# A two-layer encoder trunk on one core: sums of the activations built from their two parts in memory, a head's decay gates called behind the scores of the head ahead of it, norm and transposes placed later

## The chip, the cores and the metric

The kernel runs on one core of a Trainium2 chip. The metric is the time of one execution on the device in microseconds (us). Times of before are the median of three runs; one further execution was profiled, and every time of an instruction comes from that one.

## The reference

The input `x` is 512 tokens of 2048 features, with 16 learned meta tokens put ahead of it, so 528 tokens run through two layers:

```
for i in range(2):
    y = rmsnorm(h, pre_norm[i])
    if i == 0: y = attention_mixer(y, ...)   # 16 query heads, 8 key/value heads, 128 wide
    else:      y = gla_mixer(y, ...)         # 4 heads, key 256, value 512 wide
    h = h + rmsnorm(y, post_norm[i])
return h[:, 16:]
```

The second mixer is gated linear attention in both directions. It projects the normed activations to q, k, v, an output gate and two low-rank gates. Each direction's low-rank gate gives a log-decay per token and key feature; its running sum is `b`. A score of a query and a key is the product of `q * exp(b)` and `k * exp(-b)`, under the direction's mask. The sum over the values is normed per head, multiplied with `silu(gate)`, and projected out. All is float32.

## The kernel before

**Two parts.** A float32 product is made of three matmuls of a rounded type (F32R): each operand is split into a high part and a low part (`split`, L134 a copy on ScalarE into the rounded type, L135 a subtraction on VectorE). Weights come from memory as 512 KB units into `wraw` (2 buffers) and are split into `whi` and `wlo` (3 each). The activations that are projected lie in `uh` and `ul`, 16 tiles of 128 features by 528 tokens each. `three` (L156) issues the three matmuls, `project` (L161) a projection to 128 columns: 16 feature tiles by three matmuls for each part of the tokens (`HALVES` are two parts of 264 tokens, `REAL` the 512 without meta tokens). A projection over `HALVES` is 96 matmuls, one over `REAL` 48.

**The planner.** The order in which instructions are called is made by `Clock` (L39). Each k step of a projection advances its time by the planned length of its matmuls (`clk.step`). A side work is a generator: `clk.drive` starts it, each `yield dt` puts its next piece dt later, and it is called between two k steps when its time has come; `clk.after(dt, fn)` does so for one function. `clk.finish(h)` calls all that is due, without matmuls between, until h is done. These are planned times, in what is called planner us below. The call order is the priority of the instructions; the framework that puts them on the engines may pull one ahead that is ready sooner, and weights are called with a priority raised by 400 instructions.

**Norm between the layers.** The last tiles of the first layer's output projection are made for the first half of the tokens and then for the second. `evac` (L793) scales a result into `hs` and adds up its square (L730 on ScalarE, L732 on GpSimd). Behind a half's last tile `mean_rsqrt` (L741) sums over the partitions with a matmul by ones (L744, `ssq`, in the one bank of `ps_t`) and makes `r0`. `residual` (L748) then makes h for one of 16 tiles and one half: it loads the input h (`h0`, 5 buffers), multiplies, adds, stores h to memory (`hf_d`, L754, on GpSimd's queue), and makes `uh` (L755) and `ul` (L756), scaled with the second layer's norm weight. `residuals` (L813) calls those of the first half; `low_rank` (L766), a side work of the next projection group, calls those of the second half. `token_major` (L779) transposes four tiles for 128 tokens into a bank (L785, `ht`), squares it for the second norm (L787) into `hb` (2 buffers), copies it to `hb` (L789) and stores that as `h1_d` from the SP queue (L790). `second_norm` (L844) makes that norm from the squares: `dg`, `mrow`, `r1row`, then the low-rank gates' input (`lt`, allocated as `r0`; `lrf`, L873).

**Sums for the seven products.** Most value columns are projected with seven products in place of eight (`seven`, L218): the feature tiles are two halves and the tokens two halves, and four of the products take sums and differences of activations, T1 to T4. `combine` (L198) makes these for the feature tiles k and k + 8 in eight steps: it loads both from `hf_d` into `x` (4 buffers, of which two exist only once the norm's tiles are gone), scales them with the norm weight (L208, L209 on ScalarE), makes the differences (L211 to L213 on VectorE), and splits the result into `th` and `tl`. Beside it four projections go to memory (`to_dram`, L860): k of head 0 (two, the first one ahead of the building), q of head 0, and the first gate tile of heads 1 and 2; `kq_d` has these in slots 0 to 4. `token_rows` (L888) transposes two value columns (L896, `vps`) and stores them as `v_d` (L901); it is called whole, 1.0 planner us behind its columns.

**GLA heads.** For each head `gates(h)` (L956) makes the running sums (`pz` matmuls L972 into the one bank of `ps_m`, `z` L973, then VectorE's scans L980 to L983), `scores(h, slot)` (L1015) fourteen score blocks (`decayed` L993 makes an operand with exp, product and split; `sm` and `ss` are the matmuls of L1011 to L1013), and `outputs(h, slot)` (L1067) the product with the values, its norm (`sso`, L1095, also in `ps_m`) and the gate. The loop over heads drives `outputs(h - 1)` and `head(h)` (gates, then scores once the outputs and q are done) beside the projections of q, of the next head's k, and of the gate tiles, and calls what is left of `head(h)` at its end. In heads 1 and 2 the first gate tile is loaded (`load_gate`, L1166), the other three are projected.

Of the kernel before, what the change touches and what calls it, by code (L numbers as in the profile page):

```python
# [82 lines left out]
def hybrid_encoder(  # L83
# [21 lines left out]
    hf_d = scratch.tile([KT, P, T], F32, name="hf_d")  # L105
    kq_d = scratch.tile([6, P, T], F32, name="kq_d")
# [91 lines left out]
    def combine(th, tl, xs, src, scale):  # L198

        def load(k):  # L200
            if k < KH:
                x = xs[k % len(xs)]
                nc.sync.dma_start(out=x.rearrange("p (j t) -> p j t", j=2), in_=src[k:k + KH + 1:KH].rearrange("j p t -> p j t"))
        for k in range(len(xs)):
            load(k)
        for k in range(KH):
            x = xs[k % len(xs)]
            A.activation(x[:, :T], x[:, :T], AF.Copy, scale=scale(k))  # L208
            A.activation(x[:, T:], x[:, T:], AF.Copy, scale=scale(k + KH))  # L209
# [5 lines left out]
            load(k + len(xs))  # L215
# [532 lines left out]
    def residual(k, a, b):  # L748
        h0 = t2.tile([P, HALF], F32, tag="h0", name="h0", bufs=5)
# [4 lines left out]
        nc.gpsimd.dma_start(out=hf_d[k][:, a:b], in_=h)  # L754
# [24 lines left out]
    def token_major(k, t):  # L779
# [6 lines left out]
        hb = t2.tile([P, 512], F32, tag="hb", name="hb")[:n]  # L786
# [6 lines left out]
    def evac(ps, a, b):  # L793
        sq = squares(m, ps, a, b)
        if m == KT - 1:
            if a == 0:
                clk.after(2.0, lambda: mean_rsqrt(r0, [acc[:, a:b], sq], a, b))
                clk.after(3.5, lambda: side.append(clk.drive(residuals())))
            else:
                clk.after(1.6, lambda: mean_rsqrt(r0, [acc[:, a:b], sq], a, b))  # L800
# [43 lines left out]
    def second_norm():  # L844
# [5 lines left out]
        for t, c, n in TOK:  # L850
            dg = t2.tile([P, HALF], F32, tag="h0", name="dg", bufs=5)[:, :P]
# [104 lines left out]
    def gates(h):  # L956
# [5 lines left out]
        V.tensor_tensor(ups[32:48], ur, ups[0:16].bitcast(F32), op=ALU.subtract)  # L962
        one = ones[:, 0:1].broadcast_to([P, SEQ])
# [365 lines left out]
```

## Time and profile before

| what | value |
|---|---|
| median of three runs | 1822.78 us (1819.43 to 1823.13) |
| the profiled execution's own time | 1819.71 us |
| its span, first to last instruction | 1818.0 us |
| VectorE, ScalarE, GpSimd busy | 1063.0, 924.8, 199.3 us |
| mean granted clock of TensorE | 0.996 |
| read from and written to memory | 165.47 and 29.08 MB |

In the tables of the profile, PE is TensorE's matmuls, PEld its weight loads, DVE is VectorE, ACT ScalarE, POOL GpSimd and SP the queue that issues most transfers. An instruction's row has the source line, the engine, the operation, the tile written and the tiles read, their shapes, the count, busy us and mean ns, and then the idle time ahead of it with the instruction that ended it. Buffer numbers are left out of names, so `h0_d` and `h1_d` are both `h_d`.

### The profile page before, as it was taken

The page shows a single profiled execution, that of the slowest core. Times are in us where ns is not written, and L with a number is a line of the kernel's source. Part 1 is how long each engine was busy: PE and PEld are TensorE (multiplying, and loading weights), DVE is VectorE, ACT ScalarE, POOL GpSimd, SP SyncE. Part 2 cuts the span into 40 slices and gives each one's busy share as a digit, 9 for nine tenths or more (in the row PEclk, how much of TensorE's full clock was granted, in tenths as well). Part 3 has the DMA queues.
Part 4 walks back from the last instruction along what each step waited for, and adds up shares of the span by engine and source line. Part 5 has one row for each costly group of instructions (what it writes and reads, how often), then busy time and mean ns, then how long its engine had stood idle before and what let it go on. Part 6 is the DMA issues. An engine that isn't in the chain of part 4 may idle for free.

```text
span 1818.0 us, 32105 instructions
## 1 busy us (share of the span) xinstructions
PE 1777.5 (98%) x12711; PEld 1670.0 (92%) x12711; DVE 1063.0 (58%) x2053; ACT 924.8 (51%) x1869; POOL 199.3 (11%) x255
## 2 busy tenths in 40 slices
PE   8999999999999999999999999999999999999998
PEld 8899999999999999999999899988888888888886
DVE  5786656656565656622255667658585866854224
ACT  4554544444445454533346634459585766953221
POOL 3211111111111111111131001110000000000000
PEclk9999999999999999999999999999999999999999
DMA  8322232223333332523457644343233332344323
GB/s 254 119 59 83 82 88 82 89 83 89 84 92 86 91 112 79 171 86 90 116 165 234 191 120 117 106 135 88 77 105 88 103 93 85 101 139 170 96 93 127
DMA packets 271095, 203.13 MB, mean 112 GB/s; under 512 B 10172, under 2 KB 240640, under 8 KB 270416
## 3 DMA queue, kind: packets, MB, share of 16 engines
q1 hardware_dynamic: 262832, 175.35, 33.0%
q0 software_dynamic: 8112, 25.73, 3.8%
q8 instruction: 100, 1.64, 0.4%
q14 instruction: 51, 0.42, 0.1%
HBM read 165.47 MB, written 29.08 MB: 107 GB/s over the span
## 4 chain that ended last, share of the span: by engine, by line
PE 62%; issue 31%; POOL 3%; DVE 2%; DMA 1%; ACT 1%; SPq 0%; POOLq 0%; DVEq 0%; ACTq 0%
PE pp L157 14%; PE pp L159 14%; PE pp L158 14%; PE f L1243 2%; PE f L1241 2%; PE f L1242 2%; PE pT L581 2%; POOL v_d L901 1%; PE s L562 1%; PE s L563 1%; PE s L564 1%; PE o L602 1%; PE o L601 1%; PE o L603 1%; POOL hf_d L754 1%
## 5 line engine op out<-in xcount | busy, mean ns | idle before, releaser
L157 PE MATMUL pp<-uh,whi 128*128 128x264 f32 (+1 forms) x2640 | 803.6, 305 | 0.3 <-ACT sq L302 0.3
L158 PE MATMUL pp<-ul,whi 128*128 128x264 f32 (+1 forms) x2640 | 794.4, 301 | 0.4 <-DVE ul L429 0.4
L159 PE MATMUL pp<-uh,wlo 128*128 128x264 f32 (+1 forms) x2640 | 794.3, 301 | 0.3 <-POOL wlo L368 0.3
L159 PEld LDWEIGHTS pp<-uh,wlo 128*128 128x128 f32 x2640 | 498.1, 189 | 16.9 <-POOL wlo L368 0.6
L157 PEld LDWEIGHTS pp<-uh,whi 128*128 128x128 f32 x2640 | 497.7, 189 | 17.2 <-ACT st L900 0.8
L158 PEld LDWEIGHTS pp<-ul,whi 128*128 128x128 f32 x2640 | 498.6, 189 | 14.2 <-DVE ul L429 0.6
L135 DVE TENSOR_TENSOR wlo<-wraw,whi 128x1024 fp32r<-128x1024 f32 (+1 forms) x245 | 298.3, 1219 | 345.6 <-ACT whi L134 345.2
L134 ACT CAST whi<-wraw 128x1024 fp32r<-128x1024 f32 (+1 forms) x245 | 254.9, 1042 | 353.5 <-PE pp L158 197.6
L571 ACT ACTIVATE pn<-s,mx 128x528 f32<-128x528 f32 (+1 forms) x72 | 50.3, 698 | 88.5 <-DVE mx L568 62.9
L1243 PE MATMUL f<-whi,ul 128*128 128x512 f32 x192 | 75.6, 394 | 0.0
L1241 PE MATMUL f<-whi,uh 128*128 128x512 f32 x192 | 75.5, 393 | 0.0
L1242 PE MATMUL f<-wlo,uh 128*128 128x512 f32 x192 | 75.3, 392 | 0.0
L314 POOL TENSOR_TENSOR qw<-qw,cos 128x528 f32<-128x528 f32 x24 | 31.9, 1327 | 372.9 <-DMA qs<-qw 315.6
L567 DVE TENSOR_REDUCE mx<-s 128x1 f32<-128x528 f32 (+1 forms) x72 | 50.7, 705 | 18.4 <-PE s L564 17.2
L241 PE MATMUL pp<-th,whi 128*128 128x264 f32 x192 | 54.6, 284 | 0.0
L242 PE MATMUL pp<-tl,whi 128*128 128x264 f32 x192 | 54.6, 284 | 0.0
L243 PE MATMUL pp<-th,wlo 128*128 128x264 f32 x192 | 54.3, 283 | 0.0
L324 DVE TENSOR_TENSOR qw<-qw,qs 128x528 f32<-128x528 f32 x24 | 17.0, 706 | 60.1 <-POOL qs L315 60.1
L134 ACT CAST whi<-x 128x1024 fp32r<-128x1024 f32 x27 | 28.3, 1048 | 43.3 <-PE pp L242 21.4
L586 DVE TENSOR_TENSOR pl<-pT,ph 128x512 fp32r<-128x512 f32 (+1 forms) x80 | 47.4, 592 | 4.8 <-ACT ph L585 3.8
L585 ACT CAST ph<-pT 128x512 fp32r<-128x512 f32 (+1 forms) x80 | 40.6, 507 | 16.5 <-PE pT L581 10.4
L1104 POOL DMA_DIRECT2D og_d<-og x24 | 12.8, 540 | 326.7 <-DVE og L1102 326.7
(374 smaller groups left out, 3358.1 us busy)
## 6 DMA issues: line engine op xcount, KB each, us to landing
wraw<-in_attn_w_in_dram SPq DMA_DIRECT2D x94, 512.0 KB, 4.0
wraw<-in_gla_w_in_dram SPq DMA_DIRECT2D x81, 512.0 KB, 3.9
wraw<-in_attn_w_out_dram SPq DMA_DIRECT2D x32, 512.0 KB, 3.9
wraw<-in_gla_w_out_dram SPq DMA_DIRECT2D x32, 512.0 KB, 3.8
x<-in_gla_w_in_dram SPq DMA_DIRECT2D x15, 512.0 KB, 4.2
qs<-qw SPq DMA_DIRECT2D x96, 66.0 KB, 3.0
h<-h_d SPq DMA_DIRECT2D x32, 132.0 KB, 3.6
hf_d<-h POOLq DMA_DIRECT2D x32, 132.0 KB, 3.3
```

What stands on the lines that cost most here:

```text
L134: A.copy(hi, src)
L135: V.tensor_tensor(lo, src, hi.bitcast(F32), op=ALU.subtract)
L157: PE.matmul(ps, wh, uh[:, k, a:b], start=first, stop=False)
L158: PE.matmul(ps, wh, ul[:, k, a:b], start=False, stop=False)
L159: PE.matmul(ps, wl, uh[:, k, a:b], start=False, stop=last)
L241: PE.matmul(ps, w[0][:, k], bh[:, k], start=k == 0, stop=False)
L242: PE.matmul(ps, w[0][:, k], bl[:, k], start=False, stop=False)
L243: PE.matmul(ps, w[1][:, k], bh[:, k], start=False, stop=k == KH - 1)
L567: V.reduce_max(mx, s, axis=AX.XY)
L1241: PE.matmul(ps, uh[:, k, ts], wh[:, kk], start=(k == 0), stop=False)
L1242: PE.matmul(ps, uh[:, k, ts], wl[:, kk], start=False, stop=False)
L1243: PE.matmul(ps, ul[:, k, ts], wh[:, kk], start=False, stop=(k == KT - 1))
```

## The change

- `combine` no longer loads from memory: `x` is the sum of the two parts `uh` and `ul` of tiles k and k + 8, in one VectorE addition of 128 x 1056. The loads, the two scalings and, in `residual`, the store of h to `hf_d` go.
- The first gate tile of head 2 is projected in its head like the others; `kq_d` has four slots, and only head 1 loads its gate tile.
- `h0` has 4 buffers in place of 5, `hb` 3 in place of 2.
- `mean_rsqrt` is called 3.5 (was 2.0) and 3.2 (was 1.6) planner us behind its half, the residuals 5.0 (was 3.5).
- `token_rows` is a side work with 2.5 planner us ahead of each of its three pieces.
- `gates` waits 2.0 more behind its first copies, `scores` 1.5 more at its two first items, `outputs` 3.0 (was 1.0) ahead of `sso`.
- One generator `heads` makes gates and scores of all heads, with a slot of 4.0 (3.3 in head 3, was 3.4); the loop waits for the scores of head h - 1 when it begins head h, and starts its outputs then.

```diff
-    def combine(th, tl, xs, src, scale):
-
-        def load(k):
-            if k < KH:
-                x = xs[k % len(xs)]
-                nc.sync.dma_start(out=x.rearrange("p (j t) -> p j t", j=2), in_=src[k:k + KH + 1:KH].rearrange("j p t -> p j t"))
-        for k in range(len(xs)):
-            load(k)
+    def combine(th, tl, xs):
+
         for k in range(KH):
             x = xs[k % len(xs)]
-            A.activation(x[:, :T], x[:, :T], AF.Copy, scale=scale(k))
-            A.activation(x[:, T:], x[:, T:], AF.Copy, scale=scale(k + KH))
+            u = [t[:, k:k + KH + 1:KH].bitcast(F32) for t in (uh, ul)]
+            V.tensor_tensor(x.rearrange("p (j t) -> p j t", j=2), *u, op=ALU.add)
...
             split(th[:, k], tl[:, k], x)
-            load(k + len(xs))
             yield 2.4
...
     def residual(k, a, b):
-        h0 = t2.tile([P, HALF], F32, tag="h0", name="h0", bufs=5)
+        h0 = t2.tile([P, HALF], F32, tag="h0", name="h0", bufs=4)
...
-        nc.gpsimd.dma_start(out=hf_d[k][:, a:b], in_=h)
...
-        hb = t2.tile([P, 512], F32, tag="hb", name="hb")[:n]
+        hb = t2.tile([P, 512], F32, tag="hb", name="hb", bufs=3)[:n]
...
             if a == 0:
-                clk.after(2.0, lambda: mean_rsqrt(r0, [acc[:, a:b], sq], a, b))
-                clk.after(3.5, lambda: side.append(clk.drive(residuals())))
+                clk.after(3.5, lambda: mean_rsqrt(r0, [acc[:, a:b], sq], a, b))
+                clk.after(5.0, lambda: side.append(clk.drive(residuals())))
             else:
-                clk.after(1.6, lambda: mean_rsqrt(r0, [acc[:, a:b], sq], a, b))
+                clk.after(3.2, lambda: mean_rsqrt(r0, [acc[:, a:b], sq], a, b))
...
         for ts in ((0, 1), (2, 3), (4,)):
+            yield 2.5
             ps = ps_v.tile([P, 512], F32, tag="v", name="vps")
...
-    built = clk.drive(combine(th, tl, quarters, hf_d, lambda k: col(PRE + KT + k)))
-    clk.after(1.0, lambda ys=ys: token_rows(ys, 0))
+    built = clk.drive(combine(th, tl, quarters))
+    clk.drive(token_rows(ys, 0))
...
-    for n, h in ((3, 1), (4, 2)):
-        to_dram(n, 4096 + h * 512, 1.0, REAL)
+    to_dram(3, 4096 + 512, 1.0, REAL)
...
-        clk.after(1.0, lambda ys=ys, vc=vc: token_rows(ys, vc))
+        clk.drive(token_rows(ys, vc))
...
         V.tensor_tensor(ups[32:48], ur, ups[0:16].bitcast(F32), op=ALU.subtract)
+        yield 2.0
...
                 if d == "m":
                     made = (decayed(kf, bf, cf, 4, -1.0, SEQ, META, "km"), decayed(qf, bf, None, 4, 1.0, c, n, "q"))
+                    yield 1.5
...
-            yield 1.0
+            yield 3.0
             PE.matmul(ps, ones, acc[:, :256], start=True, stop=True)
...
-    def head(h, before):
-
-        yield from gates(h)
-        while not (before["done"] and have["q"]):
-            yield 0.5
-        side = [clk.drive(load_v(h))]
-        if 0 < h < 3:
-            side.append(clk.drive(load_gate(h)))
-        yield from scores(h, 3.4)
-        while not all(s["done"] for s in side):
-            yield 0.5
-
+    def heads():
+
+        for h in range(G_HEADS):
+            yield from gates(h)
+            while not have[h]:
+                yield 0.5
+            side = [clk.drive(load_v(h))]
+            if h == 1:
+                side.append(clk.drive(load_gate(h)))
+            yield from scores(h, 3.3 if h == 3 else 4.0)
+            while not all(s["done"] for s in side):
+                yield 0.5
+            done[h] = True
+
+    have, done = [False] * G_HEADS, [False] * G_HEADS
+    sc = clk.drive(heads())
     for h in range(G_HEADS):
-        have = {"q": False}
-        before = clk.drive(outputs(h - 1, 3.6)) if h else {"done": True}
-        sc = clk.drive(head(h, before))
+        if h:
+            while not done[h - 1]:
+                clk.pop()
+            before = clk.drive(outputs(h - 1, 3.6))
...
-        have["q"] = True
-        clk.finish(*([before] if h else []))
+        if h:
+            clk.finish(before)
+        have[h] = True
...
-        for i in range(1 if 0 < h < 3 else 0, 4):
+        for i in range(1 if h == 1 else 0, 4):
...
-        clk.finish(sc)
+    clk.finish(sc)
     clk.flush()
```

More of the change, by code (lines that the diff above doesn't have):

```diff
@@ L104, in hybrid_encoder @@
     h1_d = scratch.tile([4, P, D], F32, name="h1_d")
-    hf_d = scratch.tile([KT, P, T], F32, name="hf_d")
-    kq_d = scratch.tile([6, P, T], F32, name="kq_d")
+    kq_d = scratch.tile([4, P, T], F32, name="kq_d")
     v_d = scratch.tile([5, P, D], F32, name="v_d")
@@ L850, in second_norm @@
         for t, c, n in TOK:
-            dg = t2.tile([P, HALF], F32, tag="h0", name="dg", bufs=5)[:, :P]
+            dg = t2.tile([P, HALF], F32, tag="h0", name="dg", bufs=4)[:, :P]
             V.tensor_scalar(dg, ident, r1col[:, t:t + 1], None, op0=ALU.mult)
@@ L1167, in load_gate @@
         gr = g2.tile([P, SEQ], F32, tag="gr", name="gr", bufs=1)
-        nc.sync.dma_start(out=gr, in_=kq_d[2 + h][:, :SEQ])
+        nc.sync.dma_start(out=gr, in_=kq_d[3][:, :SEQ])
         yield 4.0
```

## The prediction

> **What bounds the kernel now.** I read the page first, then TensorE's waits, then the windows around the largest of them, then what the other engines did there. Span and busy time are these:
>
> ```profile
> span 1818.0 us, 32105 instructions
> PE 1777.5 (98%) x12711; PEld 1670.0 (92%) x12711; DVE 1063.0 (58%) x2053; ACT 924.8 (51%) x1869; POOL 199.3 (11%) x255
> ```
>
> TensorE is busy 1777.5 of 1818.0 us. A group of matmuls by itself shows how dense that is (columns of this view: window, its length, then busy us and count of PE, PEld, DVE, ACT and POOL, granted clock, DMA share, GB/s):
>
> ```profile
> 810.00:855.00 45.00, 45.00 (x372) 45.00 (x371) 9.81 (x8) 13.59 (x23) 6.77 (x7) 1.00 0.33 94
> ```
>
> 45.00 us hold 372 matmuls of 264 columns, one each 121 ns, at full clock. Work is not removed from TensorE by this change (a 48-matmul projection only moves), so what can be won is what TensorE waits for (columns: us in total, times, longest):
>
> ```profile
> PE vps L896 <- DVE y L248: 3.6, 5, 1.1
> PE ssq L744 <- issue: 2.7, 1, 2.7
> PE sso L1095 <- ACT z L973: 2.1, 3, 0.7
> PE sso L1095 <- DVE acc L1092: 2.1, 2, 1.1
> PE sm L1012 <- DVE lq L135: 2.1, 3, 1.0
> PE ht L785 <- ACT hb L787: 2.0, 1, 2.0
> PE mrow L854 <- DVE dg L852: 1.3, 1, 1.3
> PE mrow L854 <- DVE r L858: 1.0, 1, 1.0
> PE pz L972 <- DVE ups L962: 0.8, 1, 0.8
> PE plr L769 <- ACT hb L789: 0.8, 1, 0.8
> PE pz L972 <- ACT z L973: 0.8, 2, 0.5
> PE pz L972 <- DVE r L1097: 0.6, 1, 0.6
> PE ht L785 <- ACT hb L789: 0.5, 1, 0.5
> PE sso L1095 <- DVE lkm L135: 0.4, 1, 0.4
> PE ss L1011 <- ACT hq L134: 0.4, 1, 0.4
> ```
>
> All of these lie between the first layer's norm and the last GLA head, and they sum to 21.2 us. The wait of an instruction is counted from the modelled end of the one ahead (0.28 us after its start, below), while the next could have followed after 0.12 us; so a wait costs 0.16 us more than its row says.
>
> **The change, part by part.** *Third `hb` buffer, no `hf_d`.* Here is what stands behind the `ssq`, `ht`, `plr` and `mrow` waits:
>
> ```profile
> 944.65 0.60 PE L785 MATMUL ht<-ident,h 128*128 128x128 f32 x4
> 947.46 0.28 PE L158 MATMUL g<-ul,whi 128*128 128x264 f32 x1
> 950.45 0.69 PE L744 MATMUL ssq<-acc,ones 128*128 128x264 f32 x2 [2.70 <-issue]
> 948.24 0.60 ACT L787 ACTIVATE hb<-ht 128x512 f32<-128x512 f32 x1 [1.87 <-DMA h_d<-hb]
> 949.76 0.59 ACT L789 COPY hb<-ht 128x512 f32<-128x512 f32 x1
> 998.63 0.59 ACT L787 ACTIVATE hb<-ht 16x512 f32<-16x512 f32 x1 [3.18 <-DMA h_d<-hb]
> DMA to landing us min/median/max: 2.4/4.1/6.4
> 947.50:950.00 2.50, 0.25 (x3) 0.03 (x1) 0.60 (x3) 1.76 (x4) 0.54 (x1) 1.00 1.04 385
> 950.00:952.50 2.50, 2.05 (x10) 1.86 (x11) 2.50 (x5) 2.50 (x8) 0.54 (x1) 0.86 0.97 355
> 952.50:955.00 2.50, 2.50 (x14) 2.50 (x13) 1.74 (x5) 2.10 (x7) 0.00 (x0) 0.50 0.91 245
> 1002.50:1005.00 2.50, 2.12 (x6) 1.30 (x7) 1.09 (x3) 1.39 (x5) 0.72 (x2) 0.60 0.00 0
> 1005.00:1007.50 2.50, 2.50 (x17) 2.50 (x17) 0.85 (x2) 1.48 (x4) 0.56 (x2) 0.72 0.30 105
> ```
>
> ScalarE's squares of the token-major norm stood 1.87 us at 948.24 until a store of `hb` had landed (median 4.1 us, up to 6.4, with the DMA engines at a share of 1.04). Their bank is the one that `ssq` needs; the copy that empties it starts at 949.76, and `ssq` starts at 950.45, after 2.70 us. At 998.63 the same wait takes 3.18 us, with the second norm, hence `mrow`, behind it. A third buffer lets a burst of three pass without a landing, and 32 stores of `hf_d` no longer share the DMA engines. `mean_rsqrt` placed 1.6 planner us later gives the sums that much more; the residuals start 1.5 later, but VectorE's idle 1.9 us of 947.5 to 950 take that up. One `h0` buffer less may hold a residual back by a landing. So of ssq 2.7, ht 2.0 and 0.5, plr 0.8 (6.0 us) I take 5.0 and leave 1.0 for what is late next, the residuals on VectorE with that buffer. Of `mrow` the 1.3 us for `dg` go; the 1.0 us for `r` stays, because copy and product follow the matmul as before. Gain 6.3.
>
> After both waits the granted clock falls: 0.86 and 0.50, then 0.60 and 0.72, which is (0.14 x 2.5 + 0.50 x 2.5) = 1.6 us lost and (0.40 x 2.5 + 0.28 x 2.5) = 1.7 us, of the second of which some 0.4 us fall into the wait for `r`. Without the long waits I count 1.6 + 1.3 = 2.9 us won. [...] The trace halves it after 2.70 us without a start, so I keep the term.
>
> *`token_rows` in pieces, 2.5, 5.0 and 7.5 planner us behind its columns.* The transposes now wait for the last addition of `y` five times, 3.6 us. Two and a half planner us are over twice the longest, 1.1. All of it goes; the last call, in the flush, is not moved by it. Its stores on POOL's queue spread likewise, with nobody waiting for them. Gain 3.6.
>
> *Placing in the GLA heads.* This row shows the kind of wait, a `sm` matmul that stands for the split of its operand:
>
> ```profile
> 1439.59 0.29 PE L1012 MATMUL sm<-lq,hkm 128*16 128x256 f32 x1 [0.96 <-DVE lq L135]
> ```
>
> The 1.5 us for the first score item exceed the longest `sm` wait (1.0): 2.1 us go. The 2.0 us behind `ups` cover 0.8. The extra 2.0 us ahead of `sso` cover `acc` 2.1 and `lkm` 0.4. But `sso` of a first half waits for `z`, whose bank it shares: by the yields it comes 0.6 planner us after a `pz` (8.2 against 7.6) and will again (10.2 against 9.6), as both are moved by 2.0. So 2.1 stays, and pz for `z` 0.8 and ss 0.4 too. With pz for `r` 0.6 that is 6.0 us touched; I take 5.0.
>
> Tails: 15 of the waits that go (vps 5, sm 3, sso 3, pz 2, ssq, mrow) by 0.16 are 2.4 us. **Won: 6.3 + 2.9 + 3.6 + 5.0 + 2.4 = 20.2 us.**
>
> *Sums from memory.* These are the durations, the stretch from where the splits of the sums can start (the second `lrf`) to the end of the first product that reads them, and one of 512-column matmuls alone:
>
> ```profile
> L208 ACT ACTIVATE x<-x,cols 128x528 f32<-128x528 f32 x8 | 5.9, 734 | 7.6 <-DMA x<-hf_d 7.6
> L209 ACT ACTIVATE x<-x,cols 128x528 f32<-128x528 f32 x8 | 5.8, 727 | 0.0
> L135 DVE TENSOR_TENSOR tl<-x,th 128x1056 fp32r<-128x1056 f32 x8 | 10.0, 1255 | 3.5 <-ACT th L134 3.4
> L211 DVE TENSOR_TENSOR x<-x 128x528 f32<-128x528 f32 x6 | 4.1, 703 | 2.0 <-ACT x L209 2.0
> L135 DVE TENSOR_TENSOR wlo<-wraw,whi 128x1024 fp32r<-128x1024 f32 x9 | 11.0, 1219 | 1.7 <-ACT whi L134 1.7
> L865 DVE SCALAR_TENSOR_TENSOR y<-pp,r1row 128x512 f32<-128x512 f32 (+1 forms) x5 | 2.9, 582 | 0.0
> 1012.00:1063.40 51.40, 51.40 (x293) 45.03 (x293) 37.67 (x47) 27.75 (x37) 3.25 (x6) 1.00 0.65 195
> 1710.00:1755.00 45.00, 45.00 (x197) 36.68 (x196) 12.47 (x12) 11.71 (x17) 0.00 (x0) 1.00 0.30 94
> ```
>
> POOL's queue loses 32 stores, SP's eight loads and ScalarE 11.7 us; none of them ends a wait of TensorE here. VectorE gains eight additions of 128x1056. The trace has none; the nearest row is `tl`, the same size, 1.255 us, so 10.0 us. That needs room, since one projection that hid the building leaves: 197 matmuls in 45.00 us are 0.228 each, 48 of them 10.9. The window holds 37.67 us of VectorE work in 51.40. Afterwards: + 10.0, less the two additions that can run ahead of it on the two buffers that exist early (before, too, only 6 of 8 `L211` lie in it), less two weight splits 2.4 and one evacuation 0.7: 42.1 us in 51.4 - 10.9 = 40.5. VectorE is over by 1.6 us even if never idle; its groups show 7.2 us idle ahead of `tl`, `L211` and `wlo` there, part of it for the scaling that goes. TensorE will wait here, where nothing waits now: between 0 (the product walks through `th` in order and may start early) and 1.6 + 7.2 = 8.8. I take 4.0, nearer to the full queue than to the idle rows. Later products catch up.
>
> *Heads.* The planner's own arithmetic: scores take 15 x 4.0 + 2 x 1.5 = 63.0 planner us behind 22.8 of gates, 85.8, while the projections of head 0 and of head 1 amount to 73.6. So gates don't come earlier than now, and some 12.2 planner us of scores, three items, are called at once ahead of the next head's projections, twice. (Heads 2 and 3: under 2.) Queued behind them in priority are q's matmuls, `outputs` and the next gates. In the trace the order of calls isn't that on TensorE: at 947.46 runs a matmul of the group, behind the transposes of 944.65 and ahead of `ssq`, though `finish` calls `ssq` before the group. So q fills the holes, and what is left are waits like `sm` and `ss`, 0.4 to 1.0 each. Bounds: 0, and two times 12.2 x 1.05 (228 ns where the planner counts 216) = 25.7 if nothing fills. I take 3.0, six items by half a microsecond. The gate tile made in head 2 costs nothing there: the same 48 matmuls, and one load less on SP's queue.
>
> **Sum: 20.2 - 4.0 - 3.0 = 13.2 us won.** The profiled execution took 1819.71 us (span 1818.0 and 1.7 around it), so 1806.5; the median of the three is 1822.78, 3.1 us more, so 1809.6 on that scale.
>
> **Rivals.** *Nothing waits at the places that I price* (no wait at the seam, no hole at the heads): 20.2 won, 1802.6. For it: ScalarE, which VectorE waits for at the seam, loses its scaling. Against: 42.1 in 40.5. *Placing does little*: the order follows readiness, and the waits that only placing touches (3.6 + 5.0 + 2.4 = 11.0) return. Then 20.2 - 11.0 - 7.0 = 2.2 won, 1820.6. Against it: those waits repeat at 0.7 to 1.1 us each, smaller than the shifts. *Slower: the three items stand alone.* If TensorE really sits through the called-at-once scores at both boundaries, 25.7 takes the place of 3.0: 9.5 lost, 1832.3. It decides from 16.2 us for both, 8.1 each. For it speaks that ScalarE is near its limit in head 0's scores already:
>
> ```profile
> 1215.00:1260.00 45.00, 44.22 (x266) 38.01 (x266) 40.27 (x80) 41.92 (x100) 0.00 (x0) 1.00 0.34 96
> ```
>
> 41.92 of 45 us; against it the interleaving above, and that wider slots lighten just this.
>
> **How the numbers follow.** Forecast 0.65, no new waits 0.18, placing does little 0.10, slower 0.07. No change is within 0.2%, 3.6 us, about what a measurement can tell here. Forecast and the first rival are faster, with 0.02 of the third case: 0.85; same 0.08; slower 0.07. The likeliest gives 1809.6. The low end is all won plus 2 of the 3.3 us that I leave: 1800.6. Seam 8.8 with heads 7.6 would leave 3.8 won, 1819.0; the high end reaches to the case behind that, 1820.6.
>
> **What would show it.** Right: `vps`, `ssq`, `ht` and `sm` vanish from the waits, no `hb` square waits for its store, the clock stays 1.00 around 950 and 1003, `sso` for `z` stays, and a wait for `tl` appears at the first `th` product. Wrong: `vps` or `sm` still there with the same length; TensorE idle for over 8 us at a head's boundary; or `th` waits of 10 us, which would mean that VectorE is the bound from there on.

## The result and the profile after

| | median | lowest to highest | runs |
|---|---|---|---|
| before | 1821.32 us | 1819.43 to 1823.13 | 4 |
| after | 1810.31 us | 1806.41 to 1811.77 | 4 |

The ratio is 0.9936, with a 95% interval of 0.9916 to 0.9956. The kernel became 11.0 us faster, between 8.0 and 15.3 us by the interval. The forecast was 13.2 us won. The profiled execution of after took 1810.19 us, and its page begins so (busy us, share and count of each engine):

```profile
span 1808.5 us, 31995 instructions
...
PE 1774.5 (98%) x12711; PEld 1671.9 (92%) x12711; DVE 1072.4 (59%) x2061; ACT 914.9 (51%) x1853; POOL 180.6 (10%) x222
```

The span is 9.5 us shorter than before. TensorE runs the same 12711 matmuls; its busy time is 3.0 us less (1777.5 to 1774.5) and its idle time 6.5 us less (40.5 to 34.0), so about two thirds of the gain in the span are waiting that is gone. VectorE has 9.4 us more, mostly the eight additions (10.0); ScalarE has 9.9 less, mostly the scalings (11.7); GpSimd's part is 18.7 less, mostly the issues of the stores (32 of 0.54 us, 17.3). What TensorE waits for between the norm and the last head is now this (us in total, times, longest):

```profile
PE sso L1088 <- ACT z L965: 5.7, 6, 1.8
...
PE ss L1003 <- ACT hq L133: 2.4, 2, 1.2
PE ht L776 <- DVE h L745: 2.0, 2, 1.7
...
PE vps L1109 <- ACT vt L1103: 1.1, 1, 1.1
...
PE plr L760 <- ACT hb L780: 1.0, 1, 1.0
PE pz L964 <- ACT z L965: 0.8, 2, 0.5
PE sm L1004 <- DVE lq L134: 0.8, 2, 0.4
PE pz L964 <- DVE ups L953: 0.6, 1, 0.6
...
PE ht L776 <- ACT hb L778: 0.6, 1, 0.6
...
PE sm L1003 <- ACT hq L133: 0.3, 1, 0.3
```

Line numbers have moved by 7 to 9 in this part of the code: L1088 is `sso`, L1003 and L1004 are score matmuls, L776 is `ht`, L888 the transposes of `token_rows`. Gone are `vps` for `y` (3.6), `ssq` (2.7), `mrow` for `dg` and `r` (2.3), and `sso` for `acc` and `lkm` (2.5). `ht` for the square (L787 before, L778 now) fell from 2.0 to 0.6. New or longer are `sso` for `z` (2.1 to 5.7, from three times to six), `ss` for `hq` (0.4 to 2.4) and `ht` for h itself (0 to 2.0).

These are windows at the places that were shown of before (columns as there: PE, PEld, DVE, ACT, POOL, granted clock, DMA share, GB/s). The first two are the first norm's, then the second norm, the building of the sums, and two places in the heads:

```profile
947.50:950.00 2.50, 2.19 (x16) 1.91 (x16) 2.50 (x8) 2.46 (x7) 0.00 (x0) 1.00 0.82 243
950.00:952.50 2.50, 2.50 (x21) 2.38 (x20) 2.26 (x7) 2.33 (x7) 0.00 (x0) 1.00 0.97 280
1000.00:1002.50 2.50, 2.50 (x23) 2.50 (x22) 1.14 (x2) 1.05 (x1) 0.00 (x0) 1.00 0.00 0
1003.90:1044.30 40.40, 40.40 (x245) 36.14 (x246) 40.18 (x50) 18.87 (x24) 3.78 (x7) 1.00 0.46 134
1261.00:1263.00 2.00, 1.45 (x6) 1.27 (x7) 1.89 (x5) 1.32 (x3) 0.00 (x0) 0.71 0.38 91
1263.00:1265.00 2.00, 2.00 (x11) 2.00 (x11) 0.52 (x2) 0.55 (x2) 0.00 (x0) 0.50 0.63 188
1370.00:1372.00 2.00, 1.60 (x8) 1.48 (x9) 1.89 (x4) 1.18 (x3) 0.00 (x0) 0.77 0.39 96
```

The clock stays at 1.00 through both norms. In the building VectorE is busy 40.18 of 40.40 us, and TensorE 40.40 of 40.40: VectorE is as full as forecast, and nobody waits for it. In the heads the clock now falls to half twice, at places where it was full before.

This table sets the profiled executions side by side, stage by stage, in us between the starts of TensorE's instructions. The projection that moved from the building into head 2 is 48 x 0.228 = 10.9 us; the last column takes it into account.

| stage | before | after | won |
|---|---|---|---|
| first softmax score to last `lrf` (layer 1, norm) | 928.93 | 920.72 | 8.2 |
| last `lrf` to first `th` product (building) | 48.66 | 37.64 | 11.0, less 10.9 moved: 0.1 |
| first to last `th` product (seven products) | 123.58 | 119.39 | 4.2 |
| last `th` product to first `pz` | 22.47 | 22.30 | 0.2 |
| first `pz` to first `pf` (heads) | 417.65 | 431.54 | -13.9, plus 10.9 moved: -3.0 |
| first `pf` to the end (`pf` is the last projection's first tile) | 194.01 | 194.09 | -0.1 |

The gain lies in the norm and in the seven products. The heads look 3 us worse in this pair of profiles. The two stretches at half clock, 3.41 us each and so 1.7 us lost each, are 3.4 us of that; the experiments show what else is the pair.

### The profile page after: what moved, and what is told of

Read it like the earlier page. It is cut to its first block, busy times and chain, and to the rows that moved or that the text cites. A ratio compares the mean times of both kernels' runs of the same rounds, so it can differ in the third digit from the quotient of the medians.

```text
span 1808.5 us, 31995 instructions
## 1 busy us (share of the span) xinstructions
PE 1774.5 (98%) x12711; PEld 1671.9 (92%) x12711; DVE 1072.4 (59%) x2061; ACT 914.9 (51%) x1853; POOL 180.6 (10%) x222
## 4 chain that ended last, share of the span: by engine, by line
PE 62%; issue 28%; DVE 3%; ACT 2%; POOL 2%; DMA 2%; SPq 0%; POOLq 0%; DVEq 0%; ACTq 0%
PE pp L156 14%; PE pp L158 14%; PE pp L157 13%; PE f L1242 2%; PE f L1240 2%; PE f L1241 2%; PE pT L573 2%; PE s L554 1%; PE s L556 1%; PE s L555 1%; POOL v_d L893 1%; PE o L594 1%; ACT whi L133 1%; PE o L593 1%; PE o L595 1%
## 5 line engine op out<-in xcount | busy, mean ns | idle before, releaser
L134 DVE TENSOR_TENSOR wlo<-x,whi 128x1024 fp32r<-128x1024 f32 x27 | 33.0, 1222 | 19.5 <-ACT whi L133 19.5
```

The source lines that it names most:

```text
L134: V.tensor_tensor(lo, src, hi.bitcast(F32), op=ALU.subtract)
```

## Experiments

Each kernel ran three rounds beside the kernel before on the same chip. In the table, "norm" is the first stage of the table above, "building", "seven" and "heads" are its second, third and fifth; times are of the profiled executions, one for each kernel.

| kernel | ratio to before (95%) | norm | building | seven | heads |
|---|---|---|---|---|---|
| before | 1 | 928.9 | 48.7 | 123.6 | 417.7 |
| after | 0.9936 (0.9916 to 0.9956) | 920.7 | 37.6 | 119.4 | 431.5 |
| 1 before, third `hb` | 0.9985 (0.9975 to 0.9995) | 927.0 | 49.3 | 128.1 | 419.2 |
| 2 before, sums from the parts | 0.9999 (0.9988 to 1.0011) | 928.6 | 48.7 | 122.2 | 424.4 |
| 3 after, two `hb` | 0.9964 (0.9951 to 0.9977) | 931.2 | 37.5 | 119.4 | 430.7 |
| 4 after, norm as early as before | 0.9923 (0.9909 to 0.9938) | 920.0 | 37.6 | 119.7 | 432.1 |
| 5 after, `token_rows` whole | 0.9946 (0.9926 to 0.9967) | 922.2 | 37.6 | 122.4 | 429.4 |
| 6 after, additions twice | 0.9989 (0.9978 to 1.0001) | 922.8 | 42.3 | 123.7 | 432.2 |
| 7 after, heads as before | 0.9937 (0.9923 to 0.9952) | 924.0 | 37.6 | 119.5 | 432.5 |
| 8 after, gate tile by memory | 0.9958 (0.9941 to 0.9975) | 922.2 | 48.8 | 119.3 | 422.2 |
| 9 after, shorter slot | 0.9916 (0.9901 to 0.9931) | 922.4 | 37.6 | 119.5 | 428.8 |
| 10 after, `sso` in another bank | 0.9923 (0.9904 to 0.9941) | 922.7 | 37.6 | 119.5 | 432.7 |
| 11 = 4 and 9 | 0.9904 (0.9887 to 0.9920) | 919.8 | 37.6 | 119.7 | 428.9 |
| 12 = 4, 10 and later operands | 0.9879 (0.9864 to 0.9893) | 920.9 | 37.6 | 119.7 | 424.6 |

**1. The third buffer alone**, in the kernel before.

```diff
-        h0 = t2.tile([P, HALF], F32, tag="h0", name="h0", bufs=5)
+        h0 = t2.tile([P, HALF], F32, tag="h0", name="h0", bufs=4)
...
-        hb = t2.tile([P, 512], F32, tag="hb", name="hb")[:n]
+        hb = t2.tile([P, 512], F32, tag="hb", name="hb", bufs=3)[:n]
```

> The kernel before with a third hb buffer (and h0 at 4) and nothing else of the change. Theory 'buffer': the norm stage wins because a square no longer waits for the store of an hb tile; then the waits ssq 2.7, ht 2.5 and mrow dg 1.3 go, the clock stays full around 950 and 1003, and the time is 6 to 8 us under before, some 1814. Rival 'traffic': the stores of hf_d made the landings late, and the third buffer only helps with them gone; then hb squares still wait several us, and the gain is under 3 us.

The ratio is 0.9985, and the norm stage is 2.0 us shorter, not 8. The squares wait only 0.2 us for their stores (8.5 before), yet TensorE's two long waits are there as before, `ssq` at 951.55 and `ht` at 978.28. This is ScalarE's order of work in that kernel ahead of each of them (start, duration, then the wait), and TensorE's waits:

```profile
947.52 0.63 ACT L787 ACTIVATE hb<-ht 128x512 f32<-128x512 f32 x1
...
949.92 1.04 ACT L134 CAST whi<-wraw 128x1024 fp32r<-128x1024 f32 x1 [1.69 <-DMA wraw<-in_gla_w_in_dram]
950.87 0.58 ACT L789 COPY hb<-ht 128x512 f32<-128x512 f32 x1
...
974.76 0.74 ACT L208 ACTIVATE x<-x,cols 128x528 f32<-128x528 f32 x1 [1.46 <-DMA x<-hf_d]
```
```profile
PE ht L785 <- ACT hb L787: 2.8, 1, 2.8
...
PE ssq L744 <- issue: 2.5, 1, 2.5
```

The square starts without a wait at 947.52. Behind it in ScalarE's queue stands the split of a weight unit, whose transfer lands late (1.69 us), and the copy that empties the bank for `ssq` stands behind that. Ahead of the second wait, ScalarE stands 1.46 us for a load of the sums' building into `x`, and the square that empties the bank for `ht` comes behind it, at 977.57. So a landing that ScalarE no longer waits for at one instruction is followed by one that it waits for at the next. The clock fell to half behind both waits (stretches from 952.41 and 979.72; the granted clock is 0.50 in 952.5 to 955 and in 980 to 982.5). In this profile the seven products are 4.6 us longer than in before: the longest wait of `vps` is 2.3 us, and another stretch at half clock follows it (the mean granted clock of the whole profile is 0.994, that of before 0.996).

**2. The sums alone**, in the kernel before: `combine` as in after, no `hf_d`, two `hb`.

```diff
-        nc.gpsimd.dma_start(out=hf_d[k][:, a:b], in_=h)
...
-    built = clk.drive(combine(th, tl, quarters, hf_d, lambda k: col(PRE + KT + k)))
+    built = clk.drive(combine(th, tl, quarters))
```

> The kernel before with combine's sums from uh and ul, and no hf_d; two hb buffers, all placing as before, four projections beside the building. 'Buffer': the waits of hb squares for their stores stay (8.5 us of ScalarE before), gain under 3 us. 'Traffic': landings fall well under 4.1 us, the waits go, gain 5 to 8 us. Both: no wait at the first th product, since VectorE has 37.7 + 7.5 us of work in 51.4.

No change in time: 0.9999. ScalarE's squares wait as long for their own stores as before, with 32 stores fewer on the DMA engines (us, times):

```profile
  DMA h_d<-hb: 9.2, 5
...
DMA to landing us min/median/max: 2.1/3.2/6.5
```

The median landing is 3.2 us here and was 4.1, but the longest is 6.5 and was 6.4, and two buffers don't outlast that. The building took 48.7 us with the additions in it and 48.7 without, so nothing waits at the seam while the fourth projection still covers it. The load into `x` that held up ScalarE in run 1 (and for 1.41 us at 972.32 in before) is gone, and the longest `ht` wait is 0.5 us in place of 2.0. In the heads, whose code is that of before, this profile has one `sm` wait of 4.6 us and a stretch of 6.8 us at half clock that begins in it (the granted clock from 1180 to 1625 is 0.99, in before 1.00); why was not found.

**3. After with two `hb` buffers.**

```diff
-        hb = t2.tile([P, 512], F32, tag="hb", name="hb", bufs=3)[:n]
+        hb = t2.tile([P, 512], F32, tag="hb", name="hb", bufs=2)[:n]
```

> The changed kernel with two hb buffers. 'Pair': hb squares wait for stores again and 5 us or more of the 8.2 in that stretch are lost. 'Placing': about 2 us are lost, as much as the buffer won alone. In both the stretch from second lrf to the first th product and all behind it stay as they are.

The norm is 10.5 us longer than in after, and the ratio goes back to 0.9964. The store waits are back in full:

```profile
  DMA h_d<-hb: 9.4, 6
...
DMA to landing us min/median/max: 2.1/3.9/6.4
```

Runs 1 to 3 together: the buffer alone is worth 2.0 us in this stage, the absent stores and loads alone 0.3, and both (run 4, below, has just these two in the norm) 928.9 - 920.0 = 8.9. Neither is enough by itself; they work as a pair. Run 1's trace has both kinds of landing behind which the waits then stood, a weight unit's and a load's into `x`; how much each of them is worth was not separated.

**4. After with the norm placed as early as before.**

```diff
-                clk.after(3.5, lambda: mean_rsqrt(r0, [acc[:, a:b], sq], a, b))
-                clk.after(5.0, lambda: side.append(clk.drive(residuals())))
+                clk.after(2.0, lambda: mean_rsqrt(r0, [acc[:, a:b], sq], a, b))
+                clk.after(3.5, lambda: side.append(clk.drive(residuals())))
             else:
-                clk.after(3.2, lambda: mean_rsqrt(r0, [acc[:, a:b], sq], a, b))
+                clk.after(1.6, lambda: mean_rsqrt(r0, [acc[:, a:b], sq], a, b))
```

> The changed kernel with the norm's sums and the residuals called as early as before (2.0, 3.5 and 1.6). From the first softmax score to the second lrf the kernel before takes 928.9 us, the changed one 920.7; a third hb buffer alone gave 2.0 of these 8.2, the sums alone 0.3. Theory 'pair': third buffer and absent stores together give the rest, the later calls nothing; the stretch stays within 1 us of 920.7. Rival 'placing': the later calls give it; the stretch goes back to some 926, the time rises by 4 to 6 us.

The norm is not longer: 920.0. One wait stands in it, in place of after's `ht` for h, `ht` for `hb` and `plr`:

```profile
PE ssq L736 <- issue: 1.6, 1, 1.6
```

With the late placing, `ssq` finds its sums ready and the residuals, now 1.5 later, make `ht` wait. The seven kernels with the late placing, two-part sums and three buffers (after, 5 to 10) took 920.7 to 924.0, 922.4 in the mean; the three with the early placing (4, 11, 12) 919.8 to 920.9, 920.2 in the mean. So the later placing of the norm costs some 2 us in this stage, of which about 0.7 are the clock: three of the seven profiles (6, 9, 10), and none of the three, have a stretch at half clock near 955, taken at 1.7 us each. The two groups touch (after has 920.7), so the size is uncertain. In the time of the whole kernel this lies within the intervals.

**5. After with `token_rows` whole**, 1.0 behind its columns as before.

```diff
+        yield 1.0
         c = slice(vc * P, (vc + 2) * P)
         for ts in ((0, 1), (2, 3), (4,)):
-            yield 2.5
```

> The changed kernel with token_rows called whole, 1.0 planner us behind its columns, as before. Theory 'late addition': the five vps waits for y come back (3.6 us, 4.4 with tails), the seven-product stretch grows from 119.4 to 123.6 us and the time by 4. Rival 'given back': the later stretches take up what is lost; the time moves by less than 1.5 us.

The seven products are 3.0 us longer, 122.4 against 119.4, and the wait that had vanished is there again, five times:

```profile
PE vps L888 <- DVE y L240: 2.4, 5, 0.7
```

In the time of the whole kernel (0.9946) this lies within the intervals.

**6. After with every addition made twice**, 8 x 1.25 = 10.0 us more on VectorE in the building.

```diff
-            V.tensor_tensor(x.rearrange("p (j t) -> p j t", j=2), *u, op=ALU.add)
+            for _ in range(2):
+                V.tensor_tensor(x.rearrange("p (j t) -> p j t", j=2), *u, op=ALU.add)
```

> The changed kernel with each of the eight additions of uh and ul done twice (same result, 10.0 us more of VectorE, of which two additions lie ahead of the building). VectorE is busy 40.2 of the 40.4 us from the second lrf to the end of the first th product, and TensorE does not wait there. Theory 'edge': that stretch is full, so 7.5 us more on it delay the first th products by 5 to 8 us. Rival 'slack': much of what VectorE does there is work for later that moves back; TensorE waits under 2 us.

The building is 4.7 us longer and the seven products 4.3, together 9.0 for the 10.0 added. These are TensorE's waits in that stretch, VectorE's group of additions (busy us, mean ns, idle ahead), the window behind the longest wait, and two instructions of ScalarE ahead of it:

```profile
PE pp L234 <- ACT y L258: 4.5, 1, 4.5
...
PE pp L235 <- DVE tl L134: 0.9, 1, 0.9
```
```profile
L203 DVE TENSOR_TENSOR x<-uh,ul 128x1056 f32<-128x1056 f32 x12 | 15.0, 1250 | 0.0
```
```profile
1045.00:1047.00 2.00, 1.81 (x8) 1.81 (x9) 2.00 (x3) 0.14 (x1) 0.00 (x0) 0.50 0.84 225
```
```profile
1041.93 1.99 ACT L133 CAST whi<-wraw 128x1024 fp32r<-128x1024 f32 x2 [2.44 <-DVE wraw L228]
...
1044.77 0.37 ACT L258 COPY y<-pp 128x264 f32<-128x264 f32 x1
```

The waits for `y` and `tl`, with 0.5 us for `th`, are 5.9 us; behind the longest comes a stretch of 6.8 us at half clock, which costs 3.4. The theory of the edge holds in the time lost. The longest wait is not for a sum, though: by its row the first `th` product waits for ScalarE's copy L258, which starts at 1044.77 behind the casts of weights, and the first of these waited 2.44 us for a sum of weights on VectorE (L228). By its parts, of the 10.0 us added 4.1 still found room: 2.5 ahead of the building (12 of the 16 additions lie in it, 6 of 8 in after) and 1.6 in it. The rest stands in TensorE's way, with the clock on top of it. In after the same additions have no idle time ahead of them, and the last `tl` is made late. These are the group, the first `th` product, the last `tl`, and what TensorE runs then:

```profile
L202 DVE TENSOR_TENSOR x<-uh,ul 128x1056 f32<-128x1056 f32 x6 | 7.5, 1250 | 0.0
```
```profile
1041.14 0.29 PE L233 MATMUL pp<-th,whi 128*128 128x264 f32 x1
...
1043.69 0.44 PE L233 MATMUL pp<-th,whi 128*128 128x264 f32 x2
...
1045.07 0.41 PE L234 MATMUL pp<-tl,whi 128*128 128x264 f32 x2
```
```profile
1043.71 1.25 DVE L134 TENSOR_TENSOR tl<-x,th 128x1056 fp32r<-128x1056 f32 x1
```

The first `th` product starts at 1041.14, and the last `tl` ends at 1043.71 + 1.25 = 1044.96, 3.8 us behind that start. The product takes the eight pieces in turn, three matmuls each, and comes to the last one at 1043.69, before its `tl` is made. There its first matmul and the first of the next product run one behind the other (x2 in the row); nine more of the next product follow, and the one that needs the last `tl` runs at 1045.07, beside the next product's (x2 again). So two things cover the late `tl`: the order of reading, and some 1.2 us of the next product put in between.

**7. After with the heads' loop and yields of before**, and the gate tile still made in head 2.

```diff
-    def heads():
-
-        for h in range(G_HEADS):
-            yield from gates(h)
-            while not have[h]:
-                yield 0.5
...
+    def head(h, before):
+
+        yield from gates(h)
+        while not (before["done"] and have["q"]):
+            yield 0.5
...
+        yield from scores(h, 3.4)
```

> The changed kernel with the heads as before: one generator for each head, slots of 3.4, the shorter yields ahead of pz, sm and sso; sums, buffers, token_rows and the gate tile of head 2 stay as changed. From the first pz to the first output matmul the kernel before takes 417.7 us with one projection (10.9) less, which makes 428.6; the changed one takes 431.5. Theory 'heads lose': the stretch is 428 to 429 and the kernel 2 to 4 us faster than the changed one. Rival 'heads win': the waits that placing removed (sm 2.1, acc 2.1) return on top of today's, and it is 3 us slower.

The ratio stays at 0.9937 and the heads take 432.5 us, 1.0 more than in after, so the new loop with its placing loses nothing by itself (that the heads lose, as supposed until then, falls) and, in the stage's time, gains next to nothing. The waits change hands:

```profile
PE sm L1002 <- ACT hq L133: 2.2, 1, 2.2
...
PE sso L1086 <- ACT z L964: 2.1, 3, 0.7
PE pz L963 <- DVE ups L953: 2.0, 2, 1.3
PE sso L1086 <- DVE acc L1083: 1.8, 2, 1.0
```

**8. After with head 2's first gate tile by memory**, as before, and a slot of 3.2 in head 2 so that its planned sum fits.

```diff
-    to_dram(3, 4096 + 512, 1.0, REAL)
+    for n, h in ((3, 1), (4, 2)):
+        to_dram(n, 4096 + h * 512, 1.0, REAL)
...
-            if h == 1:
+            if 0 < h < 3:
                 side.append(clk.drive(load_gate(h)))
-            yield from scores(h, 3.3 if h == 3 else 4.0)
+            yield from scores(h, (4.0, 4.0, 3.2, 3.3)[h])
```

> The changed kernel with head 2's first gate tile made beside the state's building again, written to memory and read back ahead of head 2, as the kernel before does; its 48 matmuls leave head 1's softmax and stand between the last norm product and the first th product (head 2's step of the schedule is 3.2 there, so that its planned sum fits). Theory 'the tile is neutral': the 10.9 us only change place: last norm product to first th product 48.6 us instead of 37.6, the heads 431.5 - 10.9 = 420.6 us instead of 431.5, and the time is the changed kernel's within 1.5 us. Rival 'the tile costs in the heads': its matmuls and the conversions behind them crowd the heads, which come out 3 to 4 us below that, at about 417, since the kernel before has 417.65 there although with the old order of the heads and the tile in them they took 432.5, and the time is 3 to 4 us less than the changed kernel's.

The building is 48.8 us again, and the heads 422.2, nearer to 420.6 (neutral) than to 417. That the tile costs in the heads falls; where it is made doesn't matter to within the spread. The ratio, 0.9958, is if anything on the slower side of after's, and the intervals overlap.

Heads with the old loop, the tile's 10.9 us taken out, took 417.7, 419.2, 424.4 (2) and 421.6 (7), 420.7 in the mean. With the new loop they took 420.6, 419.7, 421.1, 418.5, 421.2 (after, 3, 4, 5, 6) and 422.2 (8), 420.5 in the mean. With 1.7 us taken off for each 3.41 us at half clock in the heads, the means are 419.8 and 419.1. The heads are neutral; that the profile of before had 417.7, the best of its four, and that of after two stretches at half clock, made them look 3 us worse in the pair.

**9. After with a slot of 3.2 in heads 0 and 1**, so that the scores' planned time fits beside the projections and no items are left for one call at the boundary.

```diff
-            yield from scores(h, 3.3 if h == 3 else 4.0)
+            yield from scores(h, (3.2, 3.2, 4.0, 3.3)[h])
```

> The changed kernel with a slot of 3.2 in heads 0 and 1, so that gates and scores (22.8 + 51.0 planner us) end with the head's projections (73.6) and no items are left to be called at once. Theory 'called at once': the two ss waits of 1.2 us and the two half-clock stretches of 3.4 us at 1261 and 1371 go, 4 to 6 us under the changed kernel, some 1805. Rival 'crowding': ScalarE and VectorE are the limit of the scores, and closer slots bring ss and sm waits of the same sum elsewhere; within 2 us of the changed kernel.

The heads are 2.8 us shorter, and the granted clock in them is 1.00 (from 1180 to 1625), where after has 0.99. The waits there:

```profile
PE sso L1088 <- ACT z L965: 6.1, 6, 1.8
...
PE sm L1004 <- DVE lq L134: 1.3, 3, 0.4
PE sm L1003 <- ACT hq L133: 1.3, 3, 0.6
...
PE ss L1003 <- ACT hq L133: 0.7, 1, 0.7
```

`ss` falls from 2.4 to 0.7, and `sm` rises from 1.1 to 2.6 in its place. Of the 2.8 us, the waits give little; the two half-clock stretches behind after's `ss` waits, of about 3.4 us each at half speed, were worth 1.7 each. That is not the edit's alone: in runs 3 and 5 the two `ss` waits are there, the granted clock in the heads is 1.00 in both, and they take 430.7 and 429.4, so without the clock the shorter slot wins 0.7 to 1.9 us. The time of the whole kernel (0.9916) lies at the edge of after's interval.

**10. After with `sso` in a bank of the scores**, so that it no longer shares one with `pz`.

```diff
-            ps = ps_m.tile([P, 512], F32, tag="m", name="sso")[:, :256]
+            ps = ps_s.tile([P, 512], F32, tag="s", name="sso")[:, :256]
```

> The changed kernel with the sums of squares of the outputs (sso) in a bank of the scores' pool instead of the one bank that the gates' pz use. Theory 'shared bank': all six sso waits for z (5.7 us, 6.7 with the tails) go, some 1804 to 1805. Rival 'late sums': the bank is not the last that is missing, acc comes little earlier, and waits for acc of 2 to 3 us take its place; gain under 3 us.

All 5.7 us of `sso` are gone and nothing is won: heads 432.7. The wait is at the scores:

```profile
PE sm L1003 <- ACT hq L133: 6.8, 3, 2.8
```

Freed from the bank, TensorE arrives earlier at the next block's operand, which is made no sooner. Part of the loss is the clock: three stretches at half clock stand in the heads of this profile, 1.7 us lost in each, and two in after (0.99 from 1180 to 1625 in both).

**11. Runs 4 and 9 together.**

> The changed kernel with the norm's sums called as early as before (from the first softmax score to the second lrf 920.0 us) and slots of 3.2 in heads 0 and 1 (the stretch of the heads 428.8 instead of 431.5). If both add up, 3 to 4 us under the changed kernel, some 1806. If what is won ahead is lost in waits behind, within 1.5 us of it.

Norm 919.8 and heads 428.9: both stages are as in the run that changed them alone. The median is 1806.40 us, ratio 0.9904.

**12. Runs 4 and 10 together, with the operands given time.** The slots are 3.0 (3.6 in head 2), and the first item's matmuls come 4.5 planner us behind their operands.

```diff
-                    yield 1.5
+                    yield 1.5 if half else 4.5
...
-            ps = ps_m.tile([P, 512], F32, tag="m", name="sso")[:, :256]
+            ps = ps_s.tile([P, 512], F32, tag="s", name="sso")[:, :256]
...
-            yield from scores(h, 3.3 if h == 3 else 4.0)
+            yield from scores(h, (3.0, 3.0, 3.6, 3.0)[h])
```

> The norm's sums as early as before, sso in a bank of the scores' pool, 4.5 instead of 1.5 planner us ahead of a head's first score matmuls, and slots of 3.0 (3.6 in head 2), so that the planned sum still fits. Theory 'placed too tight': the sso waits go with the shared bank (they did, but sm waits of 6.8 us came), and the sm waits go with the room ahead of them; the heads' stretch falls to some 424, the time to 1801 to 1803. Rival 'ScalarE's queue': with closer slots ScalarE is late with whatever comes next, ss or sm waits stay at 5 us or more and the stretch is 428 or more.

The median is 1802.79 us (1801.80 to 1803.50), the best of all, with an interval that lies below after's. The heads are 424.6, 6.9 less than in after. What is left of the waits there and in the norm:

```profile
PE vps L1109 <- ACT vt L1103: 2.8, 2, 2.1
PE ssq L736 <- issue: 2.3, 1, 2.3
...
PE pz L964 <- DVE ups L953: 1.2, 1, 1.2
...
PE sm L1003 <- ACT hq L133: 1.1, 1, 1.1
...
PE sm L1004 <- DVE lq L134: 1.0, 3, 0.4
```

The change of bank that won nothing in run 10 is part of this, where the operand that came next is also asked for later. Which of the three edits in the heads does how much was not separated.

## Why the prediction was right, and where it was wrong

The direction and the size were right: 1809.6 was forecast and 1810.31 measured. The sum had 13.2 us, and 11.0 came; that the times lie closer than that is because the median of before came out 1.5 us lower with its fourth run (1821.32) than the 1822.78 from which the forecast started. These are its terms, with the tails that belong to each, against what the stages measured: in the pair of profiles, and in the means over the kernels that share the code where there are several (for the norm of before there is one profile only):

| term | forecast | pair | means |
|---|---|---|---|
| norm: 5.0 + 1.3 + half clock 2.9 + tails 0.3 | 9.5 | 8.2 | 6.5 |
| seam on VectorE | -4.0 | 0.1 | 0.1 |
| `vps` 3.6 + tails 0.8 | 4.4 | 4.2 | 4.2 |
| heads: 5.0 + tails 1.3 - bursts 3.0 | 3.3 | -3.0 | 0.2 |
| sum | 13.2 | 9.5 | 11.0 |

Two terms were wrong by 4 us and by 3 to 6 us with opposite signs, and the right total owes something to that: it is luck in part.

*Third `hb` buffer, no `hf_d`: right, with two corrections.* `ssq` (2.7) and `mrow` (2.3, with the 1.0 for `r` that was to stay) went, and the clock stayed at 1.00. Of `ht` and `plr`, 3.3 us before, 3.6 are there (2.0 of them for h), where the step left 1.0. Run 1 shows what the step did not see: with the buffer alone, ScalarE's queue stands at the next landing, so the absent `hf_d` transfers are half of the cause and not a help beside it. That none of the loads ends a wait of TensorE was wrong too: the longest `ht` wait of before stood behind a load into `x`, for which ScalarE waited 1.41 us. And the step gave the later placing of `mean_rsqrt` a share of the gain; run 4 shows that it costs some 2 us, because the residuals 1.5 later make `ht` wait. The idle 1.9 us that was to take them up did not.

*`token_rows` in pieces: right.* 4.2 won of 4.4, and run 5 gives 3.0 of it back by undoing this part alone. The rest comes with the sums from memory, which the step did not see: in run 2, with `token_rows` whole, this stage is 1.4 us shorter than in before, and `vps` waits 2.2 us for `y` in place of 3.6.

*Sums from memory: the load was right, the wait wrong.* The addition was taken as 1.255 us from `tl` and is 1.250. VectorE was forecast 42.1 us in 40.5; it did 40.18 in 40.40. The step took 4.0 us of waiting between bounds of 0 and 8.8; it is 0. Two things that it named were not given their weight. VectorE's 7.2 us of idle before was all waiting for ScalarE (`th` 3.4, `x` 2.0, `whi` 1.7), whose scalings, with 7.6 us of waiting for loads of `hf_d`, go; after has none of it. And the product walks through `th` in order, so that 3.8 us of the building run behind its start, more than the 1.6 that VectorE was over by; the step named this and gave it no number. That TensorE does not wait even for the last `tl` is owed to matmuls of the next product, which the step did not see. Run 6 bounds the reserve that was left in the building: of 7.5 us more, 1.6 found room.

*Placing in the GLA heads: the step that failed most.* It had 5.0 us won. `sm` went from 2.1 to 1.1, `acc` and `lkm` went, but `sso` for `z` went from 2.1 to 5.7. The step said that the 2.1 stay, since `sso` and `pz` are moved by the same 2.0; it looked at the first halves of the heads alone. In after both halves' `sso` come behind a `z` in the shared bank, six waits in place of three, up to 1.8 us. So the 2.0 us that were to cover `acc` were waited for at the bank. Run 10 shows that this bank isn't the limit either: with `sso` out of it the waits stand at `sm`. Moving one consumer showed the next wait, for an operand that ScalarE and VectorE make no sooner. Run 12, which moves the consumers of both, is the one that wins.

*Heads, bursts: they cost about what was said, in another form.* 3.0 us were forecast for the items called at once at two boundaries, as some six waits of half a microsecond. There are two waits of 1.2 us for `hq`, 2.4 in all, and in this execution each was followed by a stretch at half clock worth 1.7 us. Run 9, which removes the bursts, has 2.8 less, of which 0.7 to 1.9 are without the clock's part.

*The rivals.* "Nothing waits at the priced places" was right at the seam and wrong in the heads. "Placing does little" was right in the heads (run 7) and wrong for `vps` (run 5). "The three items stand alone" didn't happen: q's matmuls filled in between, and the longest wait at a boundary is 1.2 us.

*What would show it.* `vps` for `y`, `ssq` and the clock's falls at 950 and 1003 are gone, `sso` for `z` stayed, as said. One square still waits for a store, 1.7 us, where none was to. `ht` still waits, for another releaser. `sm` is halved, not gone. The wait for `tl` at the first `th` product, which was to appear, did not.

## What to carry to other kernels

What ScalarE waited for in run 1 was not one landing: with 0.2 us left of 8.5 at the squares, it waited 1.69 and 1.46 us for the landings of a weight unit and of a load into `x`. So ask which landing the next instructions of such a queue stand for, and expect a buffer to help only as far as that one. Pricing an engine that gets more work than its window holds, first take out the idle time whose cause the change removes (here 7.2 us), and count the reserve that the consumer's order of reading gives (with the work of its next product, 3.8 us here). Where waits are 1 us long and repeat in a pipeline, moving the consumer can move the wait (in run 10 the 5.7 us of `sso` go and `sm` goes from 0.3 to 6.8), and a single pair of profiles with a few us of spread cannot tell which; compare the stage over several kernels that share its code.

## What the runs showed of the hardware that was not expected

The granted clock halves after waits as short as 1.2 us, and not always. This is after at the first of the two places in the heads (start, duration, wait):

```profile
1259.89 0.44 PE L156 MATMUL pp<-uh,whi 128*128 128x512 f32 x1
1261.55 0.39 PE L1003 MATMUL ss<-hq,hk 128*128 128x256 f32 x1 [1.22 <-ACT hq L133]
...
1265.12 0.35 PE L1071 MATMUL o<-al,vh 128*128 128x256 f32 x1
1265.31 0.28 PE L1072 MATMUL o<-ah,vl 128*128 128x256 f32 x1
```

From 1261.8 to 1265.2 the matmuls follow each other at half speed (the windows above have 0.71 and 0.50). In run 5 the same two `ss` waits are there with the same length, and the clock stays full (the mean of that profile is 0.999, that of after 0.995). Some longer waits were not followed by half clock: 1.73 us of `ht` at 955.67 and 1.77 us of `sso` at 1302.99 in after, 1.98 us of `ht` at 976.63 in before, each with a granted clock of 1.00 from its end on for 7 us and more. The length of the wait alone doesn't decide, then, and what does was not found.

Where the clock fell in the norm and the heads, it was at 0.50 for 3.41 us each time: in before from 951.80 and from 1003.00, in after from 1261.85 and from 1371.07. The two starts are 51.2 us apart in before and 109.2 in after, 15 and 32 times 3.41. So the `ssq` wait of before, 2.70 us, and the `ss` waits of after, less than half as long, cost the same 1.7 us of clock.

The stores of `hb` (256 KB each) land no sooner at the long end when 32 others are absent: the longest took 6.4 us before, 5.9 in after, 6.5 and 6.4 in runs 2 and 3. How long the squares waited for them went with the number of buffers: 8.5, 9.2 and 9.4 us with two (before, runs 2 and 3), and 0.2, 1.7 and 0.9 with three (run 1, after, run 4), with the 32 stores and without.
